# Forming the block sums of the last MLP's weight pairs with accumulating DMAs instead of VectorE additions

## The chip, the cores and the metric

The kernel runs on one core of a Trainium2 chip. The metric is the device time of one execution in microseconds (us). The engines named below are PE (TensorE: matmuls, and PEld: its weight loads), DVE (VectorE), ACT (ScalarE), POOL (GpSimd) and SP (SyncE, which here only issues transfers). Transfers issued by SP and by POOL go through separate queues but are moved by the same 16 DMA engines.

## The reference

A two-layer decoder trunk over 528 positions (16 learned meta tokens and 512 real ones), width 1024, all in float32. Layer 0 mixes with an mLSTM group and a gated linear recurrence, layer 1 with differential attention. Each layer ends with a squared-ReLU MLP of inner width 4096; the second of these is "the last MLP":

```
h = h + _sq_relu_mlp(_rmsnorm(h, norm_mlp[layer]), mlp_w1[layer], mlp_w2[layer])

def _sq_relu_mlp(hn, w1, w2):
    a = jax.nn.relu(hn @ w1)
    return (a * a) @ w2
```

A final RMSNorm follows, and the meta tokens are dropped.

## The kernel before

Activations lie with features on the 128 partitions and positions along the free dimension. Weights come from DRAM (`wu`) in units of 128 x 1024 float32, 512 KB each, in a fixed order `seq`. Float32 accuracy is reached by splitting every operand into a high part (`..._h`, a rounded copy that ACT writes) and a low part (`..._l`, the rest, a subtraction on DVE), and by three matmuls per product: high by high, high by low, low by high.

The first product of each MLP is computed for 26 of its 32 column groups in pairs: two units, loaded together as one 1 MB tile `rawp`, give two output groups of 128 features. A pair is a 2 x 2 block matrix product done with seven block products instead of eight (Winograd's form of Strassen's method). The seven need, beside the blocks themselves, sums of blocks. With r0, r1, r2, r3 for the four 128 x 512 quarters of `rawp`, the tile `sums` (four quarters, called `s4`) holds

```
s4[0] = r0 + r2
s4[2] = r2 + r3
s4[3] = r2 + r3 + r0
s4[1] = r2 + r3 + r0 + r1
```

The function `emit_pair` prepares a pair. It issues the load of `rawp` and puts four steps on a list `todo`: `first` splits r0 and r1 into A; `sums` forms s4[0], s4[2], s4[3] (one DVE addition of 128 x 1024, L287, and one of 128 x 512, L289) and splits s4[2:4] into S; `last` splits r3 into D; `rest` forms s4[1] (L299) and splits s4[0:2] into U. The function `feed` takes one step off the list, or emits the next load, after each step of the matrix work. The tile `sums` has one buffer, `rawp` two.

In `pair_mm` the matrix work of a pair goes g1 (A, bank X), g6 and g5 (S, banks Y and Z), g2 (A again, X), g7 and g3 (U, Y and Z), g4 (D, Y): a pair takes 84 matmuls (L333). Between pairs stand the units of the second product (`mw`, L908). In the last MLP thirteen pairs are computed: the first two directly one after the other, then one pair to two such units, the last four pairs with one unit between. The last eight units are the final quarter of the second product, computed with positions on the partitions (`mf`, L1242) and ending in the final norm and the output.

The order of work on each engine is fixed when the program is built, by a scheduler that goes by priorities and by its own costs; `soon()` and `now()` raise priorities. An engine runs its instructions in that order, so one that waits holds up all behind it. All weight loads of the MLPs are issued by SP through `load`, which puts them in one chain in program order. Tiles share SBUF bytes: where a tile takes bytes that another one used, its load waits for the last reader of those. POOL issues the transfers of `make_ahead` (the tiles `ra` and `rah`, `ral`) during the first MLP only. In the last MLP its work is the sum of squares of the norm (`nsq`, L486) at the start, and four multiplications for the output (`zg`, L1251) at the end.

Of the kernel before, what the change touches and what calls it, by code (L numbers as in the profile page):

```python
# [10 lines left out]
F32 = mybir.dt.float32  # L11
F32R = mybir.dt.float32r
AF = mybir.ActivationFunctionType
ALU = mybir.AluOpType
AX = mybir.AxisListType

P = 128
# [23 lines left out]
U_MLP1 = 161  # L41
# [40 lines left out]
for _last in (False, True):  # L82
    o = list(FIRST)
# [35 lines left out]
def trunk(tc, hT, wu, wri, pk, lv, rope, gf, out, probe=None):  # L119
    nc = tc.nc  # L120
# [6 lines left out]
    with ctx:  # L127
        cp = ctx.enter_context(tc.tile_pool(name="cp", bufs=1))
        wr = ctx.enter_context(tc.tile_pool(name="wr", bufs=2))
# [16 lines left out]
        def wide(pool, n, dt, **kw):  # L146

            return pool.tile([P, -(-n // HV) * HV], dt, **kw)[:, :n]
# [7 lines left out]
        def sub(eng, o, a, b):  # L156
            eng.tensor_tensor(out=o, in0=a, in1=b, op=ALU.subtract)  # L157
# [21 lines left out]
        def soon():  # L179
            return tc.high_priority(offset=BOOST)  # L180
# [15 lines left out]
        def in_turn(key, issue):  # L196

            with tc.issue_after(state[key].ins) if key in state else nullcontext():
                state[key] = issue()

        def load(out, in_):
            in_turn("load", lambda: nc.sync.dma_start(out=out, in_=in_))
# [63 lines left out]
        def split_w(name, raw, n=1024, bufs=N_W):  # L266
            hl = [wide(wp, n, F32R, tag=f"v{p}" if n == 1024 else f"wd{p}", name=name + p, bufs=bufs) for p in "hl"]
            nc.scalar.copy(hl[0], raw)  # L268
            sub(nc.vector, hl[1], raw, hl[0].bitcast(F32))
            return hl  # L270

        def emit_pair():
            i = state["next"]
            raw = wide(wr, 2048, F32, tag="rawp", name=f"rawp{i}", bufs=2).rearrange("p (a c) -> p a c", a=4)
            load(raw.rearrange("p (u a) c -> p u (a c)", u=2), wu[i:i + 2].rearrange("u p c -> p u c"))
            it = {}

            def first():
                with soon():
                    it["A"] = split_w(f"A{i}_", raw[:, 0:2, :])  # L280

            def sums():

                s4 = it["s4"] = wide(wr, 2048, F32, tag="sums", name=f"sums{i}", bufs=1).rearrange(
                    "p (a c) -> p a c", a=4)
                with soon():
                    nc.vector.tensor_tensor(out=s4[:, 0:4:2], in0=raw[:, 0:4:3],  # L287
                                            in1=raw[:, 2:3].to_broadcast([P, 2, 512]), op=ALU.add)
                    nc.vector.tensor_tensor(out=s4[:, 3], in0=s4[:, 2], in1=raw[:, 0], op=ALU.add)  # L289
                    it["S"] = split_w(f"S{i}_", s4[:, 2:4])  # L290

            def last():
                with soon():
                    it["D"] = split_w(f"D{i}_", raw[:, 3], 512, 1)

            def rest():
                s4 = it["s4"]
                with soon():
                    nc.vector.tensor_tensor(out=s4[:, 1], in0=s4[:, 3], in1=raw[:, 1], op=ALU.add)  # L299
                    it["U"] = split_w(f"U{i}_", s4[:, 0:2])  # L300
            todo.extend((first, sums, last, rest))
            ready.append(it)
            state["next"] += 2
# [549 lines left out]
        for t in PLAN:  # L853
            k, a = t[0], [int(c) for c in t[1:]]
# [519 lines left out]
```

## Time and profile before

| | us |
|---|---|
| median of 3 runs | 1435.83 |
| fastest and slowest run | 1435.29, 1436.41 |
| span of the profiled execution, first to last instruction | 1434.4 |
| outside that span, by the median | 1.4 |
| PE busy in the span | 1410.9 |
| DVE, ACT, POOL busy | 1004.4, 746.9, 205.9 |

The profile is of one execution. Its page gives busy time by engine and the longest groups of instructions; further views group instructions by tile, list waits, and show the busy time of each engine in chosen stretches. In the timeline view each row is: start in us, duration in us, engine, line, operation, written tile and read tiles, count, and in brackets the engine's idle time before it with what ended it. Neighbouring rows of the same kind are merged into one with their count, and matmuls overlap, so a merged row's duration isn't the engine's time for it. In the view by stretches each engine's busy time is followed by its number of instructions; the last columns are the granted clock, the share of the DMA engines' time, and GB/s.

The last MLP begins at about 1080 us of the span, its pairs run from about 1139 to 1377 us, and the final quarter follows.

### The profile page before, as it was taken

Reading aid. Unit: us, or ns where it says so; the run is one execution under the profiler, and the core shown is the slowest. Engines: PE = TensorE matmul, PEld = TensorE weight load, DVE = VectorE, ACT = ScalarE, POOL = GpSimd, SP = SyncE. Lnnn points to the kernel's source line nnn. Section 1 sums busy time; section 2 is a strip of 40 time slices with the busy share of each in tenths; the row PEclk is TensorE's granted clock in tenths of the full one; section 3 lists DMA queues with packets and bytes.
Section 4 is the critical chain, followed back from the end, with each engine's and each line's share of the span. In section 5 each row is a group of like instructions: output and inputs, shape, how many; then the busy total and the mean of one; then the engine's idle time right before and its main releaser. Section 6 shows DMA issues by size and latency. Waiting matters only on the chain. (4 is left out here: it accounts for less than half of the span.)

```text
span 1434.4 us, 25730 instructions
## 1 busy us (share of the span) xinstructions
PE 1410.9 (98%) x10282; PEld 1337.7 (93%) x10282; DVE 1004.4 (70%) x1743; ACT 746.9 (52%) x1318; POOL 205.9 (14%) x284
## 2 busy tenths in 40 slices
PE   7999999999999999999999999999999999999998
PEld 7999999999999999999999998989877898899986
DVE  4767663657645998888886468777748987767752
ACT  6455743747424556656654435565635454454552
POOL 3000001010003024445330311101002000000001
PEclk9999999999999999999999999999999999999999
DMA  7332314223123369889873275555442332333231
GB/s 231 114 114 71 101 62 125 74 82 95 60 90 118 104 226 352 301 311 327 293 260 98 110 210 167 170 173 160 126 172 78 132 118 74 103 118 103 74 118 44
DMA packets 69636, 210.19 MB, mean 147 GB/s; under 512 B 12650, under 2 KB 14199, under 8 KB 69516
## 3 DMA queue, kind: packets, MB, share of 16 engines
q1 hardware_dynamic: 53580, 157.15, 34.5%
q0 software_dynamic: 15360, 50.34, 9.4%
q8 instruction: 81, 1.33, 0.4%
q10 hardware_dynamic: 576, 1.05, 0.2%
q14 instruction: 39, 0.32, 0.1%
HBM read 162.11 MB, written 35.71 MB: 138 GB/s over the span
## 5 line engine op out<-in xcount | busy, mean ns | idle before, releaser
L229 ACT CAST wh<-raw 128x1024 fp32r<-128x1024 f32 x141 | 147.6, 1048 | 287.1 <-PE mw L908 80.9
L908 PE MATMUL mw<-ah,wl 128*128 128x264 f32 (+1 forms) x704 | 221.1, 314 | 0.0
L908 PE MATMUL mw<-al,wh 128*128 128x264 f32 (+1 forms) x704 | 220.9, 314 | 0.0
L908 PE MATMUL mw<-ah,wh 128*128 128x264 f32 (+1 forms) x704 | 220.9, 314 | 0.0
L157 DVE TENSOR_TENSOR wl<-raw,wh 128x1024 fp32r<-128x1024 f32 x134 | 163.7, 1222 | 67.4 <-ACT wh L229 62.8
L908 PEld LDWEIGHTS mw<-ah,wl 128*128 128x128 f32 x704 | 132.4, 188 | 8.4
L908 PEld LDWEIGHTS mw<-al,wh 128*128 128x128 f32 x704 | 132.4, 188 | 7.4
L908 PEld LDWEIGHTS mw<-ah,wh 128*128 128x128 f32 x704 | 132.3, 188 | 7.4
L950 DVE TENSOR_TENSOR h<-mw,h 128x264 f32<-128x264 f32 (+1 forms) x176 | 87.2, 497 | 19.9 <-PE mw L908 19.2
L333 PE MATMUL mpX<-xp,A_h 128*128 128x264 f32 (+1 forms) x416 | 77.2, 283 | 0.0
L486 POOL TENSOR_TENSOR nsq<-nsq 128x528 f32<-128x528 f32 (+1 forms) x28 | 43.7, 1561 | 185.3 <-ACT nsq L484 184.5
L333 PEld LDWEIGHTS mpX<-xp,A_h 128*128 128x128 f32 x416 | 65.0, 188 | 1.0
L157 DVE TENSOR_TENSOR al<-rt,ah 128x528 fp32r<-128x528 f32 (+1 forms) x64 | 46.3, 724 | 20.4 <-ACT ah L160 18.3
L333 PE MATMUL mpX<-xp,A_l 128*128 128x264 f32 (+1 forms) x208 | 58.8, 283 | 0.0
L1251 POOL TENSOR_TENSOR zg<-z,gfr 128x512 f32<-128x512 f32 x4 | 5.2, 1293 | 331.4 <-DVE z L1249 320.6
L1055 POOL TENSOR_TENSOR qr<-qr,tb 128x512 f32<-128x512 f32 (+1 forms) x16 | 24.4, 1525 | 165.3 <-DVE qs L1054 158.9
L918 ACT ACTIVATE rt<-rt 128x528 f32<-128x528 f32 (+1 forms) x64 | 40.7, 638 | 10.5 <-DVE rt L937 9.4
L268 ACT CAST S_h<-sums 128x1024 fp32r<-128x1024 f32 x26 | 27.3, 1051 | 36.0 <-issue 12.8
L157 DVE TENSOR_TENSOR ral<-ra,rah 128x512 fp32r<-128x512 f32 x64 | 43.6, 682 | 1.1 <-ACT rah L160 0.2
L1116 DVE TENSOR_REDUCE mx<-psc 128x1 f32<-128x264 f32 (+3 forms) x80 | 33.2, 429 | 15.1 <-PE psc L1111 7.4
L1123 ACT ACTIVATE e<-psc,mx 128x264 f32<-128x264 f32 (+3 forms) x80 | 38.2, 481 | 9.3 <-DVE mx L1116 8.3
L160 ACT CAST ah<-rt 128x528 fp32r<-128x528 f32 (+1 forms) x64 | 40.0, 626 | 2.8 <-DMA part135h<-rah 0.9
(817 smaller groups left out, 4402.0 us busy)
## 6 DMA issues: line engine op xcount, KB each, us to landing
raw<-wu SPq DMA_DIRECT2D x141, 512.0 KB
rawp<-wu SPq DMA_DIRECT2D x26, 1024.0 KB
ra<-wu POOLq DMA_DIRECT2D x64, 256.0 KB, 5.7
h<-hT SPq DMA_DIRECT2D x16, 264.0 KB
st<-rh SPq DMA_DIRECT2D x32, 132.0 KB
kz<-rl SPq DMA_DIRECT2D x16, 132.0 KB
st<-rh SPq DMA_DIRECT2D x16, 128.0 KB
st<-rl SPq DMA_DIRECT2D x16, 128.0 KB
```

Of the source, the lines that this page charges most:

```text
L157: eng.tensor_tensor(out=o, in0=a, in1=b, op=ALU.subtract)
L160: nc.scalar.copy(hl[0][:, sl], src)
L229: nc.scalar.copy(wh, raw)
L268: nc.scalar.copy(hl[0], raw)
L333: nc.tensor.matmul(st[b][:, :hv], ww[:, cc], xx, start=st[b, "n"] == 0, stop=k == 3 and j == 2, skip_group_check=True)
L486: state["kz"] = nc.gpsimd.tensor_tensor(out=fin[0][:, lo:], in0=fin[0][:, lo:], in1=sq[:, lo:], op=ALU.add)
L908: nc.tensor.matmul(ps, w[ww], x[xx][:, tk], start=k == j == 0, stop=k == len(ws) - 1 and j == 2)
L918: nc.scalar.activation(out=t[:, cols], in_=t[:, cols], func=AF.Square)
L950: nc.vector.tensor_tensor(out=hf, in0=ps, in1=hf, op=ALU.add)
L1055: pool_or_dve("mM"[w]).tensor_tensor(out=raw[:, lo:], in0=raw[:, lo:], in1=tb[0][:, lo:], op=ALU.mult)
L1116: nc.vector.tensor_reduce(out=mx[:, 2 * c + r:2 * c + r + 1], in_=d[:, :m], axis=AX.X, op=ALU.max, negate=True)
L1123: nc.scalar.activation(out=e[:, s0:s0 + m], in_=d[:, :m], func=AF.Exp, bias=mx[:, 2 * c:2 * c + 1], accum_out=ss[:, c + 2 * r:c + 2 * r + 1])
```

## The change

For pairs of the last MLP (`far`, unit index at or above `U_MLP1`) the tile s4 is not computed on DVE. It is loaded four times with r2, by one transfer in the chain of loads on SP directly behind the pair's `rawp` load (1 MB written). Four accumulating transfers, issued by POOL in a chain of their own (`acc`), then add to it from DRAM: r3 to quarters 1, 2 and 3; r0 to quarters 1 and 3; r0 to quarter 0; r1 to quarter 1. Each must wait for what it adds to. The steps `sums` and `rest` keep only their splits. The tile is a new one, `sumd`, with two buffers. The first MLP's pairs are unchanged.

```diff
@@ emit_pair
             raw = wide(wr, 2048, F32, tag="rawp", name=f"rawp{i}", bufs=2).rearrange("p (a c) -> p a c", a=4)
             load(raw.rearrange("p (u a) c -> p u (a c)", u=2), wu[i:i + 2].rearrange("u p c -> p u c"))
             it = {}
+            far = i >= U_MLP1
+            if far:
+                s4 = it["s4"] = wide(wr, 2048, F32, tag="sumd", name=f"sums{i}", bufs=2).rearrange(
+                    "p (a c) -> p a c", a=4)
+                r0, r1, r2, r3 = (wu[i + a // 2][:, a % 2 * 512:a % 2 * 512 + 512] for a in range(4))
+
+                def over(r, n):
+                    return r.rearrange("p (a c) -> p a c", a=1).to_broadcast([P, n, 512])
+                load(s4, over(r2, 4))
+                for o, r in ((s4[:, 1:4], over(r3, 3)), (s4[:, 1:4:2], over(r0, 2)), (s4[:, 0], r0), (s4[:, 1], r1)):
+                    in_turn("acc", lambda: nc.gpsimd.dma_start(out=o, in_=r, accum_op=ALU.add))
...
             def sums():
 
+                if far:
+                    with soon():
+                        it["S"] = split_w(f"S{i}_", it["s4"][:, 2:4])
+                    return
...
                 with soon():
-                    nc.vector.tensor_tensor(out=s4[:, 1], in0=s4[:, 3], in1=raw[:, 1], op=ALU.add)
+                    if not far:
+                        nc.vector.tensor_tensor(out=s4[:, 1], in0=s4[:, 3], in1=raw[:, 1], op=ALU.add)
                     it["U"] = split_w(f"U{i}_", s4[:, 0:2])
```

## The prediction

> **What bounds the kernel now.** I read the page first, then the busy time by stretch over the last MLP, then what PE waited for there, then the tile `sums`, then the timelines around the first pair and around one in the middle.
>
> ```profile
> span 1434.4 us, 25730 instructions
> PE 1410.9 (98%) x10282; PEld 1337.7 (93%) x10282; DVE 1004.4 (70%) x1743; ACT 746.9 (52%) x1318; POOL 205.9 (14%) x284
> ```
>
> PE is busy for 98% of the span, DVE for 70%. The stretches, before the pairs (1080 to 1120), at the first pairs (1120 to 1160), and the rest:
>
> ```profile
> 1080.00:1120.00 40.00, 37.43 (x158) 28.92 (x157) 33.16 (x42) 20.43 (x28) 7.43 (x5) 1.00 0.22 75
> 1120.00:1160.00 40.00, 39.98 (x250) 35.70 (x248) 38.81 (x50) 22.35 (x32) 0.00 (x0) 1.00 0.42 143
> 1160.00:1434.40 274.40, 267.76 (x1655) 239.41 (x1653) 175.89 (x253) 125.98 (x194) 5.17 (x4) 0.99 0.27 93
> 1400.00:1434.40 34.40, 27.76 (x152) 23.60 (x150) 8.40 (x25) 8.69 (x22) 2.81 (x3) 0.93 0.12 46
> ```
>
> PE (first engine column) idles 40 - 37.43 = 2.57 us before the pairs and 0.02 us in the 40 us at the first pairs. Of the last 274.40 us it idles 6.64, all of it after 1400 us (34.40 - 27.76), in the final quarter and the output. What it waited for from 1080 us on:
>
> ```profile
> PE mn L908 <- DVE nx3l L457: 0.7, 1, 0.7
> PE mn L908 <- DVE nx5l L457: 0.7, 1, 0.7
> PE mn L908 <- DVE nx6l L457: 0.7, 1, 0.7
> PE mn L908 <- DVE nx4l L457: 0.3, 1, 0.3
> ```
>
> These are the parts of the norm's input, before any pair. No pair's matmul waited for a sum for longer than this view counts. So DVE time taken away buys almost nothing by itself; what counts is whether the new sums arrive before PE needs them.
>
> **What is removed.** The additions, in the last MLP alone:
>
> ```profile
> L287 DVE TENSOR_TENSOR sums<-rawp x13: 1215/1225/1227, 1135.2 to 1343.3; 128x1024 f32<-128x1024 f32 x13
> L289 DVE TENSOR_TENSOR sums<-sums,rawp x13: 680/681/692, 1137.0 to 1345.1; 128x512 f32<-128x512 f32 x13
> L299 DVE TENSOR_TENSOR sums<-sums,rawp x13: 681/691/695, 1138.2 to 1347.0; 128x512 f32<-128x512 f32 x13
> ```
>
> 1.225 + 0.681 + 0.691 = 2.60 us a pair, 33.8 us in 13 pairs, all beside PE work. On the path: 0. The splits S and U stay.
>
> **What is added, and its price.** Per pair: one 1.05 MB load by SP, and POOL's accumulating transfers of 0.786, 0.524, 0.262 and 0.262 MB. The issues themselves are small: SP's row for a `rawp` load below is some 0.4 us, and POOL's row for a 256 KB load is 0.54 us. POOL has nothing queued behind them that matters: after `nsq` its next instruction stands idle for 304 us.
>
> ```profile
> 1391.76 1.28 POOL L1251 TENSOR_TENSOR zg<-z,gfr 128x512 f32<-128x512 f32 x1 [304.02 <-DVE z L1249]
> ```
>
> No accumulating transfer is in this trace. Nearest are POOL's own loads of 0.262 MB and the fastest stretch of SP's loads (its last column is GB/s):
>
> ```profile
> L258 POOL DMA_DIRECT2D ra<-wu x64: 536/541/748, 462.2 to 724.4; - x64
> DMA to landing us min/median/max: 2.9/5.7/8.1
> 1124.00:1129.00 5.00, 5.00 (x23) 4.03 (x22) 4.72 (x9) 1.24 (x1) 0.00 (x0) 1.00 1.02 403
> ```
>
> At 403 GB/s 0.262 MB move in 0.65 us, so 2.9 - 0.65 = 2.25 us of the least landing time is fixed. Lower bound: an accumulated byte costs as much as a copied one: 2.25 + 0.786/0.403 = 4.2 us for the first, 3.55 for the second, 2.9 for the small ones. Upper bound: every 0.262 MB takes the loaded median 5.7 us, so 17.1, 11.4, 5.7, 5.7. I take the fixed part and twice the bytes, since what is added to must also be read: 6.15, 4.85, 3.55, 3.55. This is nearest to the row of the unloaded load, and the last MLP's transfers leave 58 to 73% of the DMA engines' time free (0.42 and 0.27 busy above), unlike the stage in which `ra` was loaded.
>
> (The Trainium skill has a rule that speaks against this change: "Collectives: The Full Stack", section "The bandwidth ceiling: the fold count and why AG ≠ RS ≠ AR", says that an add in the transfer engines halves the rate because it reads two sources, and not because adding costs cycles. By it the transfers would cost what I take; by the copy rate, the lower bound. No run here shows it.)
>
> The dependences make a chain: `rawp`, then r2 four times, then the first accumulation, then the second, which completes s4[2:4] and releases S; the fourth, which waits for the second, completes s4[1] and releases U. POOL issues in order, so the next pair's first accumulation stands behind this pair's fourth, and so behind its second landing.
>
> **In the middle.** The sixth pair's load, its splits of S and U, and PE's first matmul on S:
>
> ```profile
> 1198.33 0.43 SPq L202 DMA_DIRECT2D rawp<-wu  x1
> 1220.97 1.05 ACT L268 CAST S_h<-sums 128x1024 fp32r<-128x1024 f32 x1 [1.55 <-issue]
> 1227.79 1.05 ACT L268 CAST U_h<-sums 128x1024 fp32r<-128x1024 f32 x1
> 1234.77 0.40 PE L333 MATMUL mpY<-xp,S_h 128*128 128x256 f32 x2
> 1198.00:1219.00 21.00, 21.00 (x134) 18.89 (x133) 15.07 (x20) 9.83 (x15) 0.00 (x0) 1.00 0.30 101
> ```
>
> `rawp` and s4 together are 2.1 MB, 5.2 us at 403 GB/s; with about 1 us around them s4 has landed 6.6 us after the issue. S is whole at 6.6 + 6.15 + 4.85 = 17.6 us, U at 17.6 + 3.55 and one more small transfer's 1.3 us, 22.5. ACT came to S_h after 22.6 us and to U_h after 29.5, PE to S after 36.4. Both are in time, by 5 us on ACT and by more on PE: cost 0. If that cover is gone, ACT stands at S_h and holds up the relu and the squares behind it; at the upper bound S is whole after 35 us. The load on the DMA engines: a period of 21 us moved 101 x 21 = 2.1 MB; now 2.1 + 1.05 + twice 1.83 = 6.8 MB, 17 us of 21 at 403 GB/s, or 12.4 at the lower bound. It fits. SP's `raw` loads share this, and go out over 18 us ahead of their casts:
>
> ```profile
> 1193.58 4.70 SPq L202 DMA_DIRECT2D raw<-wu  x2
> ...
> 1212.31 1.05 ACT L229 CAST wh<-raw 128x1024 fp32r<-128x1024 f32 x1 [4.50 <-PE mw L908]
> ```
>
> **At the first two pairs there is no such room.** Their loads, ACT's rows and PE's:
>
> ```profile
> 1113.19 0.33 SPq L202 DMA_DIRECT2D raw<-wu  x1
> 1121.65 2.47 SPq L202 DMA_DIRECT2D rawp<-wu  x2
> ...
> 1137.70 1.05 ACT L268 CAST S_h<-sums 128x1024 fp32r<-128x1024 f32 x1 [5.74 <-DVE sums L289]
> 1139.07 1.05 ACT L268 CAST U_h<-sums 128x1024 fp32r<-128x1024 f32 x1 [0.32 <-PE mw L908]
> 1140.03 1.04 ACT L268 CAST A_h<-rawp 128x1024 fp32r<-128x1024 f32 x1
> ...
> 1140.30 0.40 PE L333 MATMUL mpY<-xp,S_h 128*128 128x256 f32 x2
> 1143.42 0.40 PE L333 MATMUL mpX<-xp,A_h 128*128 128x256 f32 x2
> 1144.85 0.41 PE L333 MATMUL mpY<-xp,U_h 128*128 128x256 f32 x2
> 1150.58 0.40 PE L333 MATMUL mpY<-xp,S_h 128*128 128x256 f32 x2
> 1122.00:1124.00 2.00, 2.00 (x10) 1.62 (x9) 2.00 (x2) 1.26 (x2) 0.00 (x0) 1.00 0.51 106
> ```
>
> The first `rawp` is issued at 1121.65 and PE is at its S at 1140.30, 18.65 us later; the DVE backlog already made that split just in time. After the change 0.21 MB has moved by 1124, and the first 2.1 MB by 1124 + 1.89/0.403 = 1128.7. The first accumulation then shares the engines with the second pair's `rawp` and s4 (2.1 MB more behind it on SP's queue): 6.15 us becomes some 9, landing near 1138. The second lands at 1138 + 4.85 = 1142.9, S_h is written by 1143.9: 3.6 us after PE is ready for it. The second pair: its first accumulation is issued at about 1143.5, behind the fourth of the first pair, and lands with the two small ones beside it (2 x 1.3 us) near 1151; its second at 1155.9; S_h at 1156.9 against 1150.58, so 6.3 us late, 2.7 more than the first pair's stall has already moved PE. U of the second pair (1159.5) is then in time. That is 6.3 us, less what PE can do meanwhile: the second half of A's products (1143.42 to 1144.85, 1.4 us) doesn't need S, if the order lets it go ahead. I take 5 us. The third pair's r2 load must wait for a `sumd` buffer, until the first pair's U is split, but PE comes to its S only after two second-product units, 21 us on; cost 0.
>
> Bounds of this term: at copy price S is whole at about 1138.5 and 1148.2, both before PE needs it, so 0; with every 0.262 MB at 5.7 us the first pair alone is 17 us late.
>
> **The sum.** 1434.4 - 0 + 5 + 0 = 1439.4 us of span; the median of the runs lies 1.4 us above the span shown, so 1441 us.
>
> **The rivals.** *The chain fits, no change*, about 1436. For it: at copy price there is no stall, and the first `rawp` was itself issued late, for one wait:
>
> ```profile
> SPq L202 <- PE mn L908: 8.1, 1, 8.1
> ```
>
> Between the `raw` load at 1113.19 and that `rawp` at 1121.65 SP waited 8.1 us for matmuls to finish with bytes that `rawp` was to take over. The new tiles change who takes over whose bytes; without that wait the whole chain starts up to 8 us sooner, more than the 6.3 it lacks. Against it: the same wait can as well fall on s4. It decides where the chain gains over 5 us.
>
> *The accumulation itself is the bound.* POOL's chain holds one pair's first and second transfer in a row, 11 us of a 21 us period by my price, but 28.5 at the upper bound; then each of the ten later pairs adds up to 7.5 us: 1441 + 75 = 1516, and anything from 1450 on for prices in between. It decides from a price at which those two take more than 21 us, that is twice mine. Nothing in the trace speaks for it but that `ra` median, from a stage with busier DMA engines.
>
> *Faster.* DVE is the busiest after PE at the first pairs, 38.81 of 40 us, and loses 5.2 us of work there, so the scheduler may place the norm's and the pairs' splits earlier. PE's idle time before the pairs, 2.57 us, is all that this can win: 1433.3, and just within what can be told apart. More needs the final quarter too, where no addition was removed.
>
> **How the numbers follow.** A measurement of this kernel can tell about 0.2%, 2.9 us, from no change. Late at the first pairs 0.48; no change 0.34; bound by the accumulation 0.09; faster 0.09, mostly a new order of work, as the packing and the order both change. Late by over 2.9 us or bound: slower 0.56; same 0.35; faster 0.09. The time is that of the first, 1441, its own range 1438 to 1449. The range down to 1434 takes in the no-change case, up to 1452 the beginning of the third.
>
> **What would show it.** PE waits for S_l or S_h of the first two pairs, 3 to 6 us in all, and ACT before S_h; none later. The 13 additions gone from DVE, 33.8 us less busy. Accumulations landing in 6, 5 and 3.5 us when alone, a DMA share near 0.8 in the middle periods. Wrong if POOL waits on its own transfers all through the MLP with PE idle in every period, or if the first `rawp` and r2 load go out well before 1121 us and no PE wait remains.

## The result and the profile after

| | before | after |
|---|---|---|
| median, us | 1435.89 | 1495.02 |
| fastest and slowest run, us | 1435.29, 1436.41 | 1493.29, 1498.11 |
| span of the profiled execution, us | 1434.4 | 1493.4 |
| granted TensorE clock, mean | 0.997 | 0.987 |

The change makes the kernel slower by 4.2%: the ratio is 1.0415, with a 95% interval of 1.0402 to 1.0428. The forecast was 1441 us, with 1452 as the upper end. From the page after, its first lines:

```profile
span 1493.4 us, 25867 instructions
PE 1423.9 (95%) x10282; PEld 1345.2 (90%) x10282; DVE 969.3 (65%) x1704; ACT 744.5 (50%) x1318; POOL 262.4 (18%) x336
```

DVE lost 1004.4 - 969.3 = 35.1 us of work, as meant. The span grew by 59.0 us. PE's idle time went from 23.5 to 69.5 us, 46.0 more, and its busy time by 13.0 for the same 10282 matmuls. By stretches, in the columns explained above:

```profile
1080.00:1120.00 40.00, 37.50 (x158) 28.97 (x157) 33.10 (x42) 20.35 (x29) 7.81 (x5) 1.00 0.22 76
1120.00:1160.00 40.00, 30.19 (x157) 26.34 (x157) 21.79 (x27) 11.58 (x14) 6.20 (x6) 0.87 0.86 230
1160.00:1493.40 333.40, 291.56 (x1750) 257.71 (x1748) 158.01 (x237) 134.69 (x211) 54.83 (x51) 0.96 0.70 179
1459.00:1493.40 34.40, 27.48 (x151) 23.40 (x150) 8.41 (x25) 8.68 (x22) 2.64 (x3) 0.95 0.12 46
```

Nothing is lost before 1120 us, nor in the last 34.4 us (6.9 us idle there, 6.6 before). At the first pairs PE idles 9.8 of 40 us, where it idled 0.02. How late PE comes to its first matmul on S of each pair, against the kernel before, in us from the timelines of PE:

| pair | 1 | 2 | 3 | 4 | 5 | 6 | 7 | 8 | 9 | 10 | 11 | 12 | 13 |
|---|---|---|---|---|---|---|---|---|---|---|---|---|---|
| late | 10.3 | 18.1 | 30.3 | 30.3 | 30.2 | 31.2 | 34.1 | 36.6 | 39.4 | 42.8 | 52.9 | 57.8 | 57.8 |

Three losses, then: 30 us at the first three pairs, 12 to 13 in the middle, 15 in the last four pairs, where only one unit stands between two pairs. The waits from 1080 us on:

```profile
PE mpY L349 <- ACT S_h L268: 15.5, 2, 9.8
PE mpY L349 <- DVE c L356: 11.6, 5, 4.8
PE mw L924 <- DVE c L356: 7.7, 1, 7.7
PE mpY L349 <- DVE hh L356: 6.3, 6, 1.3
...
POOL sums L287 <- DMA sums<-wu: 237.8, 28, 42.9
ACT S_h L268 <- DMA sums<-wu: 111.2, 11, 17.2
DVE S_l L157 <- ACT S_h L268: 98.8, 13, 11.7
```

PE waits for S itself only twice. ACT waits for the sums eleven times, 10 us each, DVE behind it, and most of PE's waits are for `c` and `hh`, evacuations of PSUM banks (reads of PE's finished results) that have nothing to do with the sums, but stand behind S_l on DVE. The start, in the timeline by engine (SP, POOL, ACT, PE):

```profile
1121.40 0.38 SPq L202 DMA_DIRECT2D rawp<-wu  x1
...
1157.19 0.38 SPq L202 DMA_DIRECT2D sums<-wu  x1
1175.26 2.24 SPq L202 DMA_DIRECT2D raw<-wu  x2
...
1131.03 1.37 POOL L287 DMA_DIRECT2D sums<-wu  x1 [42.91 <-DMA sums<-wu]
1140.40 2.14 POOL L287 DMA_DIRECT2D sums<-wu  x2 [8.00 <-DMA sums<-wu]
...
1167.80 2.16 POOL L287 DMA_DIRECT2D sums<-wu  x2 [6.22 <-DMA sums<-wu]
...
1149.53 1.04 ACT L268 CAST S_h<-sums 128x1024 fp32r<-128x1024 f32 x1 [17.15 <-DMA sums<-wu]
1154.86 1.05 ACT L268 CAST U_h<-sums 128x1024 fp32r<-128x1024 f32 x1 [4.00 <-DMA sums<-wu]
1155.81 1.05 ACT L268 CAST A_h<-rawp 128x1024 fp32r<-128x1024 f32 x1
...
1150.63 0.80 PE L349 MATMUL mpY<-xp,S_h 128*128 128x256 f32 x2 [9.81 <-ACT S_h L268]
1168.68 0.79 PE L349 MATMUL mpY<-xp,S_h 128*128 128x256 f32 x2 [5.69 <-ACT S_h L268]
```

The first accumulation takes from 1131.0 to 1140.4, the second (issued with the third, hence x2) to 1149.5. ACT stands at S_h for 17.15 us, and the split of the *second* pair's A, done at 1140.03 before, waits until 1155.81 behind S_h and U_h. The third pair's r2 load can't go before 1157.19, when U_l of the first pair is written. The next `raw` load goes out later still, at 1175.26, but not for the r2 load's sake: it goes at the end of a subtraction `wl` on DVE, and that stands behind the second pair's U_l. Nor did the third pair's accumulations wait for r2: by the records of the transfers POOL issued the first at 1168.40, right behind the second pair's fourth (both are in the row of 1167.80). They complete S at 1189.0, and on DVE S_l stands before the `c` for which PE waits 7.7 us (DVE, then PE):

```profile
1174.02 1.22 DVE L157 TENSOR_TENSOR wl<-raw,wh 128x1024 fp32r<-128x1024 f32 x1
1190.13 1.23 DVE L157 TENSOR_TENSOR S_l<-sums,S_h 128x1024 fp32r<-128x1024 f32 x1 [10.29 <-ACT S_h L268]
1192.97 0.41 DVE L356 TENSOR_TENSOR c<-mpY,hh 128x256 f32<-128x256 f32 x1
1193.44 0.80 PE L924 MATMUL mw<-ah,wh 128*128 128x512 f32 x1 [7.70 <-DVE c L356]
```

In the middle, the load of one pair and what follows it:

```profile
1228.60 0.92 SPq L202 DMA_DIRECT2D rawp<-wu  x1
1229.70 0.41 SPq L202 DMA_DIRECT2D sums<-wu  x1
1242.31 1.28 POOL L287 DMA_DIRECT2D sums<-wu  x1 [8.78 <-DMA sums<-wu]
1249.87 2.14 POOL L287 DMA_DIRECT2D sums<-wu  x2 [6.28 <-DMA sums<-wu]
1261.45 1.05 ACT L268 CAST S_h<-sums 128x1024 fp32r<-128x1024 f32 x1 [11.80 <-DMA sums<-wu]
```

The r2 load is in after 12.6 us, the first accumulation 7.6 us later, the second 11.6 after that: ACT has S's sums 32.9 us after the `rawp` load was issued. Before, it split S after 22.6.

### The profile page after: what moved, and what is told of

Same layout as the page of the kernel before. It is cut to its first block, busy times and chain, and to the rows that moved or that the text cites. A ratio compares the mean times of both kernels' runs of the same rounds, so it can differ in the third digit from the quotient of the medians.

```text
span 1493.4 us, 25867 instructions
## 1 busy us (share of the span) xinstructions
PE 1423.9 (95%) x10282; PEld 1345.2 (90%) x10282; DVE 969.3 (65%) x1704; ACT 744.5 (50%) x1318; POOL 262.4 (18%) x336
## 5 line engine op out<-in xcount | busy, mean ns | idle before, releaser
L287 POOL DMA_DIRECT2D sums<-wu x52 | 55.8, 1201 | 270.9 <-DMA sums<-wu 237.8
L966 DVE TENSOR_TENSOR h<-mw,h 128x264 f32<-128x264 f32 (+1 forms) x176 | 86.9, 498 | 23.5 <-PE mw L924 22.8
L157 DVE TENSOR_TENSOR S_l<-sums,S_h 128x1024 fp32r<-128x1024 f32 x26 | 31.8, 1223 | 100.0 <-ACT S_h L268 99.9
L268 ACT CAST S_h<-sums 128x1024 fp32r<-128x1024 f32 x26 | 27.3, 1048 | 138.0 <-DMA sums<-wu 111.2
L349 PE MATMUL mpY<-xp,S_h 128*128 128x264 f32 (+1 forms) x208 | 41.3, 296 | 19.2 <-ACT S_h L268 15.5
L349 PEld LDWEIGHTS mpY<-xp,S_h 128*128 128x128 f32 x208 | 33.9, 199 | 20.1 <-ACT S_h L268 15.9
L349 PE MATMUL mpY<-xp,D_h 128*128 128x264 f32 (+1 forms) x208 | 40.5, 292 | 7.9 <-DVE c L356 7.9
L157 POOL TENSOR_TENSOR wl<-raw,wh 128x1024 fp32r<-128x1024 f32 x6 | 14.8, 2459 | 183.2 <-ACT wh L229 142.1
```

The lines of the kernel that those rows point to most:

```text
L287: in_turn("acc", lambda: nc.gpsimd.dma_start(out=o, in_=r, accum_op=ALU.add))
L349: nc.tensor.matmul(st[b][:, :hv], ww[:, cc], xx, start=st[b, "n"] == 0, stop=k == 3 and j == 2, skip_group_check=True)
L966: nc.vector.tensor_tensor(out=hf, in0=ps, in1=hf, op=ALU.add)
```

## The experiments

The theory after this reading: the sums come too late for their place in the order of ACT and DVE, and the delay feeds on itself. The rivals: the crowded DMA engines (0.80 to 0.86 busy in most stretches of 40 us) make every load late; or the accumulation's rate is the bound.

**The price of one accumulation (x_price).** The kernel before, with sixteen transfers on POOL one after the other behind the output: copies of 256, 512, 768 and 1024 KB, accumulations of the same, and all again.

```diff
+ for add in (False, True, False, True):
+     for n in range(1, 5):
+         in_turn("acc", lambda: nc.gpsimd.dma_start(
+             out=q[:, 0:n], in_=r.to_broadcast([P, n, 512]), **({"accum_op": ALU.add} if add else {})))
```

> The kernel before, with sixteen transfers by POOL added behind the last output, one after the other, each waiting for the one before: plain copies of 256, 512, 768 and 1024 KB from DRAM, then accumulations of the same sizes, and both once more. Only their own landing times matter. If an accumulated byte costs twice a copied one: 2.9, 3.6, 4.2, 4.9 us for the copies and 3.6, 4.9, 6.2, 7.5 us for the accumulations, and the 7 to 11 us in the changed kernel are then contention. If the accumulation itself is dearer: above 7 us for 768 KB and above 8.5 for 1024 KB even with nothing beside it.

The second round, in POOL's timeline (each issue waits for the one before to land):

```profile
1484.23 0.72 POOL L1274 DMA_DIRECT2D quiet<-wu  x1 [2.71 <-DMA quiet<-wu]
1488.80 0.76 POOL L1274 DMA_DIRECT2D quiet<-wu  x1 [3.85 <-DMA quiet<-wu]
1493.90 0.75 POOL L1274 DMA_DIRECT2D quiet<-wu  x1 [4.34 <-DMA quiet<-wu]
1499.77 0.91 POOL L1274 DMA_DIRECT2D quiet<-wu  x1 [5.12 <-DMA quiet<-wu]
1504.21 1.21 POOL L1274 DMA_DIRECT2D quiet<-wu  x1 [3.53 <-DMA quiet<-wu]
1510.25 1.25 POOL L1274 DMA_DIRECT2D quiet<-wu  x1 [4.83 <-DMA quiet<-wu]
1518.12 1.26 POOL L1274 DMA_DIRECT2D quiet<-wu  x1 [6.62 <-DMA quiet<-wu]
```

From issue to landing, by the records of the transfers: copies 3.02, 4.29, 4.81, 5.58 us (first round 3.19, 4.51, 5.00, 5.90), accumulations 4.15, 5.75, 7.41, 8.57 (4.14, 5.85, 7.12, 8.58). The slope from 256 to 1024 KB is (8.57 - 4.15) / (5.58 - 3.02) = 1.73 times that of the copies, or 0.786 MB / 4.42 us = 178 GB/s; the fixed part is 4.15 - 0.262/0.178 = 2.7 us. So alone, S's two transfers take 7.4 + 5.75 = 13.2 us; in the kernel, from the first issue to the second landing, 17 to 21 in ten of the thirteen pairs and 13 to 15 in three. By the expectation's bounds (above 7 us for 768 KB, above 8.5 for 1024) the accumulation itself is dearer than twice the bytes at 403 GB/s; the copies are dearer than forecast too, at 0.786 MB / 2.56 us = 307 GB/s. What sharing adds in the kernel comes on top.

**Copies in place of accumulations (x_plain).** The sums are left out; the bytes brought in are the same.

```diff
- nc.gpsimd.dma_start(out=o, in_=r, accum_op=ALU.add)
+ nc.gpsimd.dma_start(out=o, in_=r)
```

> The changed kernel with its four accumulating transfers made plain copies: same bytes written, same issues, same waits, only nothing is added (the sums are left out). Theory of the long chain (S comes too late for its place in ACT's order, because accumulating is dear): S comes some 17 us after the pair's load, earlier than the 22.6 of before, so 1436 to 1441 us, what is left being the first two pairs. Theory of full transfer engines: the share falls from 0.84 to about 0.6 and the time falls too, to 1436 to 1445. If the chain of four dependent transfers is what is dear, whatever they do, the time stays above 1470.

Measured 1451.36 us (1450.69 to 1452.23), ratio 1.0111 (1.0095 to 1.0126). The 15 us are all lost at the first three pairs; from the fourth on PE keeps a constant 14.3 us behind. That is more than both theories expected, and less than the 1470 us and above that would have shown the chain of four transfers, whatever they do. So what accumulating adds makes all of the later loss, and about half of the start's 30. Whether by the length of the transfers or by the engines' time this run can't tell, since with copies the DMA engines' share falls to between 0.65 and 0.79; x_early, below, can.

**The r2 load alone (x_noacc).** No accumulation at all, and so no sums.

```diff
- in_turn("acc", lambda: nc.gpsimd.dma_start(out=o, in_=r, accum_op=ALU.add))
+ pass
```

> The changed kernel with the r2 load alone: the four accumulating transfers are left out, and so the sums. Theory (the sums come too late for their place in the order on ACT and DVE): the r2 load lands some 10 us after the load of rawp, ahead of ACT's place for S_h (22.6 us), so no wait: 1434 to 1440 us, and no row of S_h waiting for a DMA above 3 us. Rival (the extra megabyte in SP's chain delays the loads behind it): most of the loss stays, 1460 or more. The plain copies gave 1451, all lost at the first three pairs; if those 14 us are lost here too, the r2 load alone makes them.

1436.71 us (1434.79 to 1437.77), ratio 1.0007 (0.9998 to 1.0017). The extra megabyte a pair in SP's chain costs nothing.

**The first two pairs on DVE (x_third).** They use the additions again, the other eleven pairs the transfers.

```diff
- far = i >= U_MLP1
+ far = i >= U_MLP1 + 16
```

> The changed kernel, with the first two pairs of the last MLP left as before (sums on VectorE), the other eleven by accumulating transfers. In the changed kernel PE is 30 us late at the third pair and 58 at the last. If these are two separate losses: 30 us less, about 1465 us. If the late start only uses up slack that the middle would lose anyway: 1480 to 1495. If all comes from the start: 1436 to 1445.

1466.91 us (1465.91 to 1469.95), ratio 1.0222 (1.0207 to 1.0237). The start's loss is gone (the third pair's S is met at 1171.5, before 1171.6), 31 us remain. The two parts add up: 28 at the start, 31 behind it. This kernel is the base of the next ones.

**The same work, one pair earlier (x_early).** The r2 load and the accumulations of each pair are issued right behind the `rawp` load of the pair before, by a function `sum_up`; `sumd` has three buffers.

```diff
+ later = [p for p in sorted(PAIRS) if p > i and p >= U_MLP1 + 16][:1]
+ for n in ([i] if far else []) + later:
+     if ("s4", n) not in state:
+         state["s4", n] = sum_up(n)
```

> As the run with the first two pairs on VectorE, but the load of r2 and the four accumulations of each pair are issued right behind the load of the pair before it, a period of 21 us sooner, with three buffers instead of two. The bytes are the same. Theory of the long chain: S is ready long before ACT comes to it, no wait of ACT for it and 1436 to 1441 us. Theory of full transfer engines: it costs as much as without the lead, 1460 or more.

1435.37 us (1433.88 to 1436.5), ratio 0.9997 (0.9988 to 1.0007): the kernel before. Its stretch from 1160 to 1360 us, and under it that of x_third:

```profile
1160.00:1360.00 200.00, 200.00 (x1279) 181.03 (x1278) 119.03 (x163) 94.92 (x136) 41.67 (x39) 1.00 0.92 234
```

```profile
1160.00:1360.00 200.00, 184.31 (x1120) 164.87 (x1119) 101.38 (x143) 82.39 (x120) 37.67 (x35) 0.97 0.85 216
```

The DMA engines are *busier* (0.92 against 0.85) and PE doesn't idle at all, although the first accumulation takes 10.3 to 12.1 us here and the second 5.6 to 9.6. Neither full DMA engines nor the accumulation's rate cost anything in this stretch, if the chain starts early enough. In the last four pairs the lead is just used up: S of the last is complete at 1353.40, and ACT splits it at 1353.55.

**The first two pairs alone, started early (x_start).** Only these two use the transfers; their r2 loads and accumulations are issued among the `raw` loads of the first units of the last MLP.

```diff
+ far = U_MLP1 <= i < U_MLP1 + 16
...
+ if state["next"] in (U_MLP1 + 3, U_MLP1 + 5):
+     n = U_MLP1 + (10 if state["next"] == U_MLP1 + 3 else 12)
+     state["s4", n] = sum_up(n)
```

> The complement: only the first two pairs' sums by transfers, the other eleven by VectorE, and the two pairs' r2 loads and accumulations issued some units earlier, among the raw loads of the first units of the last MLP, before the loads of rawp. Theory of the lead: the start's loss of some 28 us goes too: 1434 to 1440 us. Rival (at the start the loads are short of engine time, so 5.8 MB more are late wherever they stand): 1450 or more.

1437.52 us (1435.14 to 1438.4), ratio 1.0009 (1.0000 to 1.0018). The start's loss, too, was one of lead. The two r2 loads go out at 1068.2 and 1076.6 us here, and S's sums of both stand at 1110.7, before the first `rawp` load is issued.

**A little earlier (x_lead1).** As x_third, but the r2 load and the accumulations are issued in front of the last `raw` load ahead of the pair.

```diff
+ if state["next"] + 1 in PAIRS and state["next"] >= U_MLP1 + 15:
+     state["s4", state["next"] + 1] = sum_up(state["next"] + 1)
```

> As the kernel whose first two pairs use VectorE (1466.9 us, ACT waiting 74.3 us for S's sums in 8 waits), but the r2 load and the accumulations are issued one unit earlier, in front of the last raw load ahead of the pair, some 2 to 5 us sooner. Theory of the lead: the sooner start shortens each wait by as much, so the 31 us of loss fall to between 8 and 22: 1444 to 1458 us. Rival (the DMA engines' time is the bound): no start helps, about 1467.

1449.94 us (1446.99 to 1451.15), ratio 1.0096 (1.0081 to 1.0111), in the expected range, but not as expected: up to the tenth pair nothing is lost (its S is met at 1318.5, before 1318.9), the whole loss is in the last four pairs. There POOL's timeline shows the bound:

```profile
1309.48 2.23 POOL L280 DMA_DIRECT2D sums<-wu  x2 [9.07 <-DMA sums<-wu]
1318.14 2.14 POOL L280 DMA_DIRECT2D sums<-wu  x2 [6.43 <-DMA sums<-wu]
1329.35 2.16 POOL L280 DMA_DIRECT2D sums<-wu  x2 [9.07 <-DMA sums<-wu]
```

Each row holds two issues (the second and third accumulation of a pair, then its fourth with the first of the next). A pair takes 1329.35 - 1309.48 = 19.9 us of POOL's chain, back to back, where a pair's period in the kernel before is 15.5 us.

**The middle alone (x_mid).** x_lead1, with transfers for the seven pairs between which two units stand, and DVE additions for the last four, too.

```diff
- far = i >= U_MLP1 + 16
+ far = U_MLP1 + 16 <= i < U_MLP1 + 44
```

> The r2 load and accumulations in front of the last raw load (1449.9 us with eleven pairs), but only for the seven pairs in the middle, between which two units of the second product stand; the first two and the last four pairs use VectorE. Theory: the 14 us that were left are all made by the last four pairs, whose period is 15.5 us and shorter than POOL's chain of 18 to 20 us: 1434 to 1440 us. Rival (the crowded DMA engines cost everywhere): 1444 or more.

1436.05 us (1435.37 to 1437.3), ratio 1.0003 (0.9994 to 1.0013). A start 4.2 us ahead of `rawp` is all that the middle pairs lacked.

**Transfers that nobody reads (x_unread).** x_third, with S and U split from `rawp`, so that the sums are left out and no engine waits for them.

```diff
- it["S"] = split_w(f"S{i}_", it["s4"][:, 2:4])
+ it["S"] = split_w(f"S{i}_", raw[:, 2:4])
```

> All transfers stay as they are in the kernel whose first two pairs use VectorE (1466.9 us), but the splits of S and U read rawp instead of the tile that the transfers fill, so nobody waits for them (the sums are left out of the result). Theory (the loss is ACT and DVE standing at the splits, with everything behind them in their order): 1434 to 1440 us. Rival (the transfers crowd the DMA engines and make the other loads late): about 1460 to 1467, with PE still waiting for c and hh.

1497.18 us (1495.31 to 1497.72), ratio 1.0426: the theory's expectation missed. SP's waits tell why:

```profile
SPq L202 <- DMA sums<-wu: 224.2, 11, 28.1
```

A tile that nobody reads is free as soon as it is written, and each next one took its bytes: each r2 load waited for the last accumulation of the pair before, and the `raw` and `rawp` loads stood behind it on SP. So the run doesn't answer its question. It shows the second way to lose: PE met S of the eighth pair at 1276.0 (before 1276.8) with all accumulations under way, and fell behind only when SP's chain had.

**Another order on ACT and DVE (x_order).** x_third, with S split behind D and behind the pair before's last evacuation and relu (`t4`, issued in g4).

```diff
- with soon():
+ with soon(), tc.issue_after(state["t4"].ins):
      it["S"] = split_w(f"S{i}_", it["s4"][:, 2:4])
...
- todo.extend((first, sums, last, rest))
+ todo.extend((first, last, sums, rest) if far else (first, sums, last, rest))
```

> As the kernel whose first two pairs use VectorE (1466.9 us, 31 us lost), with the same transfers at the same places, but the split of S put later in ACT's and VectorE's order: behind the split of D and behind the pair before's last bank evacuation (c) and its relu, which is some 5 us later on ACT. Theory (the loss is made by what stands behind the waiting split, not by PE lacking S): the 31 us fall by half or more, 1437 to 1454 us, and PE's waits for c and hh go. Rival (the loss is the lateness of the sums themselves or of the loads): unchanged, 1460 to 1470.

1462.83 us (1459.26 to 1464.5), ratio 1.0182: 4 us better than x_third, where 13 to 30 were expected. PE's waits for `c` fell from 15.5 to 8.8 us, but waits for `hh` (ACT and DVE) took their place, and S was still split every 23.3 us (1209.07, 1232.47, 1255.23, 1279.53, 1302.28). What stands behind the waiting split can't be the whole cause: it moved, and the pace stayed.

**Both (x_both).** The order of x_order with the lead of x_lead1.

```diff
+ if state["next"] + 1 in PAIRS and state["next"] >= U_MLP1 + 15:
+     state["s4", state["next"] + 1] = sum_up(state["next"] + 1)
...
+ with soon(), tc.issue_after(state["t4"].ins):
      it["S"] = split_w(f"S{i}_", it["s4"][:, 2:4])
```

> The later place of S's split in the order, and the r2 load and accumulations in front of the last raw load (which alone left 1449.9 us). Theory: the two give some 5 us of room each, so the sums are in time and nothing is left: 1434 to 1441 us. Rival (a floor from the crowded DMA engines remains): 1445 or more.

1450.11 us (1447.59 to 1451.41), ratio 1.0097, where 1434 to 1441 were expected: as x_lead1 alone, with the loss again in the last four pairs. The order is worth nothing there either.

**What sets the pace (x_dose).** The pace that the order left alone suggested a loop. In x_third, two rows of ACT and between them what leads from one to the other, a subtraction on DVE, SP's loads of the pair two further on and its first accumulation:

```profile
1209.77 1.05 ACT L268 CAST S_h<-sums 128x1024 fp32r<-128x1024 f32 x1 [11.57 <-DMA sums<-wu]
1219.66 1.22 DVE L157 TENSOR_TENSOR wl<-raw,wh 128x1024 fp32r<-128x1024 f32 x1
1220.90 2.14 SPq L202 DMA_DIRECT2D raw<-wu  x2
1223.09 0.91 SPq L202 DMA_DIRECT2D rawp<-wu  x1
1237.67 1.28 POOL L287 DMA_DIRECT2D sums<-wu  x1 [8.42 <-DMA sums<-wu]
1256.97 1.05 ACT L268 CAST S_h<-sums 128x1024 fp32r<-128x1024 f32 x1 [13.12 <-DMA sums<-wu]
```

S_h of the fifth pair; behind it on ACT and DVE the splits of a `raw` unit, whose end (1219.66 + 1.22) lets SP's next `raw` load go; 13.3 us after S_h the `rawp` load of the seventh pair, and its r2 load behind it, for which POOL waits; and 33.9 us behind the `rawp` load, S_h of the seventh: 47.2 us for two pairs, against 42.0 in the kernel before (1220.97 to 1262.98). To test this, one more accumulation is put between the first and the second (one quarter gets r0 once too often):

```diff
- for o, r in ((s4[:, 1:4], over(r3, 3)), (s4[:, 1:4:2], over(r0, 2)), ...
+ for o, r in ((s4[:, 1:4], over(r3, 3)), (s4[:, 3], r0), (s4[:, 1:4:2], over(r0, 2)), ...
```

> As the kernel whose first two pairs use VectorE (1466.9 us), with one more accumulating transfer of 256 KB between the first and the second, onto a quarter that the second adds to (that quarter of the sums gets r0 once too often). It lengthens the chain of each pair by some 5 us. In that kernel S_h of pair n is followed by the load of rawp n+2 after 13 to 15 us, and S_h of n+2 comes 33 us behind that: 47 us for two pairs, 23.5 a pair, where the kernel before takes 21.05. Theory (a loop over two pairs: late sums hold ACT, ACT holds the buffers, the buffers hold SP's next load of r2): 2.5 us more a pair, a period of 26 us in the middle, and 1482 to 1500 us. Rival (each pair pays its own lateness): 5 us more a pair, a period of 28.5, 1505 or more. Rival (POOL's chain alone sets the pace): the period equals the time between the first accumulations of two pairs with POOL never waiting for r2.

```profile
1216.57 1.05 ACT L268 CAST S_h<-sums 128x1024 fp32r<-128x1024 f32 x1 [13.49 <-DMA sums<-wu]
1229.90 0.48 SPq L202 DMA_DIRECT2D rawp<-wu  x1
1268.04 1.05 ACT L268 CAST S_h<-sums 128x1024 fp32r<-128x1024 f32 x1 [13.32 <-DMA sums<-wu]
```

1497.99 us (1497.5 to 1498.76), ratio 1.0433. From the fifth to the tenth pair S_h comes every (1348.52 - 1216.57) / 5 = 26.4 us, in x_third every (1325.67 - 1209.77) / 5 = 23.2: 3.2 us more a pair for an extra transfer that takes 3.9 to 9.0 us of the chain in the sixth to tenth pair, 6.1 on average. S_h to load takes 13.3 us as before; the load to S_h 38.1 instead of 33.9. Half the extra length a pair, as the loop over two pairs has it, and not the whole. The other rival, POOL's chain alone, this run doesn't exclude: between one pair's last transfer and the next pair's first, POOL waits at most 2.6 us here from the fifth pair on, so that the longer chain nearly fills the period by itself. In x_third it doesn't: POOL waits 7.5 to 8.4 us for the fifth, seventh and ninth pair and at most 2.4 for the sixth, eighth and tenth. So there every other pair starts late for its load, along the loop, and the one after it stands right behind it on POOL, or nearly.

## Why the prediction was wrong

*The direction and the place of the first loss were right, the size was not.* 1441 us came out of a term of 5 us at the first two pairs and of zeros elsewhere. By x_third the start costs 28, and the zeros 31.

*The removed additions.* 33.8 us forecast, 35.1 measured on DVE, worth nothing on the path. Right. No wait went from PE before 1120 us either, so the "faster" rival had nothing to win.

*The price of the accumulations: mis-sized, and summed as if each had the engines to itself. This is the step that failed.* 6.15, 4.85 and 3.55 us were taken; alone they take 7.4, 5.75 and 4.15. The fixed part is 2.7 us instead of 2.25, and the added bytes move at 178 GB/s instead of half of 403. The Trainium skill ("Collectives: The Full Stack", section "The bandwidth ceiling: the fold count and why AG ≠ RS ≠ AR") says that an add halves the rate; measured here it is 1.73 times the copies' slope, so nearly that. The larger error is the step after: they were summed as if alone. The text saw the sharing for the first pair's first transfer (6.15 "becomes some 9": it took 9.1) and not for the second (4.85 forecast, 9.0 measured), beside which the third, issued 0.8 us behind it, and SP's loads are under way; how much each of these adds isn't separated.

*"Both are in time ... cost 0", in the middle, is where it cost most.* s4 was to have landed 6.6 us after the `rawp` load was issued; POOL's first accumulation, which waits for it, came 10 to 16 us after the r2 load's own issue. S whole after 17.6 us became 25 to 35, against ACT's 22.6. The measured r2 load alone, with lone prices behind it (12.6 + 7.4 + 5.75 = 25.8 us), would already have been late. In x_unread, where the r2 load goes out ahead of the `raw` and `rawp` loads and behind the last accumulation, the first accumulation follows it after 6.5 to 7.6 us in the second to ninth of its eleven pairs. So the company in which a transfer lands was the larger part, and not its size. The text named the consequence ("ACT stands at S_h and holds up the relu and the squares behind it") and gave it no price. And it took ACT's place and SP's loads for fixed, so that a chain late by some 3 us would cost at most 3 us once: the rows of x_third show that the delay returns through the `raw` buffers to SP's next loads and renews itself every two pairs.

*"It fits": right, and beside the point.* 17 of 21 us of the DMA engines were forecast, that is 0.81; the shares measured are 0.80 to 0.86. x_early runs at 0.92 and loses nothing. The time available was compared with a rate, where the start of the chain was what lacked.

*The first two pairs.* S_h of the first was forecast for 1143.9 (written) and came at 1150.6. The first accumulation landed at 1140.1 instead of 1138, and 4.1 us more are the second's. For the second pair the forecast's own sum is 1.3 us short: 1143.5 + 6.15 + twice 1.3 is 1152.3 and not 1151, so its prices give 7.6 us late and not 6.3. The text let A's split of that pair stay at 1140.03; it stands behind S_h and U_h of the first pair on ACT, at 1155.81, though PE didn't wait for it.

*The third pair.* "Must wait for a `sumd` buffer ... cost 0" was right for the wait itself, which POOL and the `raw` loads don't feel, as the rows above show. What the text left out is POOL's order: the third pair's accumulations start only behind the second pair's, at 1168.40, and end at 1189.0. From the second pair's S to the third's, PE lost another 12.2 us, of which 8.2 are waits (7.70 for `c`, 0.47 for S_l). Of the rest, an estimated 2.8 go with a granted clock of 0.50, at which PE is busy for 6.3 us there (last section).

*The rivals.* "No change" rested on SP's 8.1 us wait going; it stayed (7.5 us), and the first `rawp` went out at 1121.40 instead of 1121.65. It rested on the copy price too, which was to cost nothing at the first two pairs; x_plain has copies and loses its 14.3 us there. "The accumulation itself is the bound" had a range, 1450 to 1516, that holds the time, but its rule (first and second transfer over 21 us) isn't what decided: they took 13 to 21 us, and in x_early 16 to 21 without loss. Its mechanism is shown in the last four pairs, where x_lead1 has POOL's chain at 19.9 us for a period of 15.5; the forecast reckoned with 21 us for all.

*What would show it.* PE waits for S of the first two pairs were there, 15.5 us in place of 3 to 6. "None later" failed for ACT before S_h: 111.2 us in eleven waits.

What stays open: how much of the second accumulation's landing time, 8 to 12 us in most pairs, is due to the third and how much to SP's loads; and whether POOL's chain or the loop sets the period of 26.4 us in x_dose. Which buffer makes SP wait is not open, although the wait view names `hh`, `wl` and `D_l` by turns: in x_third, from 1172 to 1318 us, each `raw` load goes out within 0.1 us of the end of a `wl` on DVE.

## What to carry to other kernels

Moving arithmetic from an engine with room into a chain of transfers trades throughput for latency: price the chain from issue to last landing, with its own transfers overlapping, and compare that with how early its first load can be issued, not with the share of the DMA engines that is free. If the consumer then waits, look at what stands behind it on its engine *and* at which loads wait for the buffers that those instructions release; where that path leads back to the chain's own load, a small lateness becomes a longer period. If such a chain is wanted, start it a stage earlier: here that alone made 1466.9 us into 1435.4, which is no gain over the additions, since DVE wasn't the bound.

## What the runs showed of the hardware

After some of its idle times PE runs slower for some microseconds. In the kernel after, behind the 9.81 us wait for the first pair's S, and in x_third behind a wait of 2.05 us that ends at 1261.46 (the third column from the end is the granted clock):

```profile
1150.60:1155.40 4.80, 4.77 (x22) 4.77 (x23) 1.23 (x1) 0.80 (x2) 1.74 (x2) 0.50 0.75 111
1155.60:1160.00 4.40, 4.40 (x40) 4.40 (x39) 3.45 (x5) 1.64 (x3) 0.54 (x1) 1.00 0.85 173
```

```profile
1261.40:1264.70 3.30, 3.24 (x15) 3.27 (x16) 1.89 (x4) 3.24 (x5) 0.00 (x0) 0.50 1.05 178
```

In the kernel after, three matmuls take 0.64 us (1154.00 to 1154.64) before 1155.4 and 0.36 us (1155.49 to 1155.85) behind it, so at the clock of 0.50 PE goes at some 0.56 of its rate. The Trainium skill ("TensorE: Matmul & The Clock Gate", section "HAM oscillation — how this bites in real kernels") puts the limit at idle gaps of about 3.4 us. These runs don't agree: single waits of 2.05 and 2.01 us in x_third were followed by it too, while 2.60 us in x_dose and 1.21 us in x_order were not, so the length of the wait alone doesn't decide. In the kernel after, PE is busy for some 19 us at this clock in the last MLP; at 0.56 of the rate that is, by estimate, 8 to 9 of the 13.0 us added to its busy time. The others aren't placed.

A transfer's landing time grows with its neighbours at least as much as with its size: the accumulations of 256 to 768 KB land after 4.15 to 7.4 us alone. In the kernel after, the two of 256 KB take 3.8 to 12.9, and the view of the tile `sums` has over all four

```profile
DMA to landing us min/median/max: 3.8/8.1/12.9
```

The accumulating issue holds POOL longer than the copying one, 0.91 to 1.26 against 0.59 to 0.77 us in x_price.
